# Decoder trunk on one core: the second mixer's causal mask moves from TensorE into VectorE's minimum, and its key-value latent is projected in plain fp32

## The chip, the cores and the metric

The kernel runs on one core of one Trainium2 chip. Its time is device microseconds (us) from one launch, the median of three runs. A profile of one further execution gives the span between the first and the last instruction, the busy time of each engine, and a record of each instruction. The engines are TensorE (PE, with PEld for its weight loads), VectorE (DVE), ScalarE (ACT), GpSimd (POOL), and SyncE (SP), which here only issues transfers.

## The reference, cut to what matters

Two layers, each a half-step SwiGLU FFN, a token mixer and another half-step FFN, for 256 tokens of width 1024 in float32. The first layer's mixer is a block-sparse attention with a learned bias (MoBA); the second layer's is a latent attention (MLA). Both have 16 heads. Only the second mixer changes:

```python
def mla_shared_kv(x, c_act, kv_ada_w, kv_ada_b, kv_norm_g, w_dkv, ...):
    hs = modulate(rms_norm(x, kv_norm_g), shift, scale)
    ckv_kpe = hs @ w_dkv                      # 256 x 1024 @ 1024 x 288
    ckv = rms_norm(ckv_kpe[..., :256], kv_a_norm_g)
    kpe = ckv_kpe[..., 256:]
    k_nope = (ckv @ w_uk).reshape(B, S, 16, 64)
    v = (ckv @ w_uv).reshape(B, S, 16, 64)
    ...
def mla_attention(h, w_dq, q_a_norm_g, w_uq, q_g, w_o, k, v, positions):
    q = (rms_norm(h @ w_dq, q_a_norm_g) @ w_uq).reshape(B, S, 16, 96)   # 1024 x 384, then 384 x 1536
    ...
    s = einsum("bqhd,bkhd->bhqk", q, k) * 96 ** -0.5
    s = where(kpos <= qpos, s, -1e30)
    o = einsum("bhqk,bkhd->bqhd", softmax(s), v)
    return o.reshape(B, S, 1024) @ w_o
```

## The kernel before

The work is one long list of instructions for the five engines. Tokens form two row tiles (`t` = 0, 1) of 128. Nearly every product is made of three fp32r matmuls: each float32 operand is split into a high part (`hi`, written by ACT) and a low part (`lo`, the rest, subtracted by DVE), and `mm3` (L799 to L803) issues hi·hi, lo·hi and hi·lo into the same PSUM bank. Weights come from HBM in the order of `weight_tiles` into a ring of three buffers (`raw`), and `wload` splits them, up to 1024 columns at a time, by an ACT copy (L678) and a DVE subtraction (L679). Modulation vectors (`ada`) are streamed through three further buffers (`adaw`).

The second mixer is `mla`. For each row tile it projects the normalized input `h` to the query latent (384 columns, L1478, records of `mm<-hi,h`) and the input `hkv`, which has its own norm and modulation, to the key-value latent (288 columns, `mm<-hi,hkv`). `q_norm`, run when the FFN before the mixer closes a row tile, has `modulate_cols` transpose the normalized rows (L850) and write `h` and `hkv`, each as a high and a low part by `split_evac` (ACT L815, DVE L816); before that split, the modulated `hkv` values stand in a tile `z`, which shares four buffers with the rows `y` to be transposed. `lat_norm_T` (L1438 to L1451) normalizes a latent, transposes it (L1448) and splits it into `qlT` or `ckT`. Then four groups `g` of four heads follow: `proj` makes their queries (`qn`) and keys (`kn`), `head_rstd` (ACT L1172, DVE L1175 and L1176, POOL's power at L1177) their norms, `to_T` transposes them (L1513), and `attention` scores, normalizes and applies them.

In `attention` a group has three score banks: `t` = 0 with four heads of 128 keys, and `t` = 1 with two banks of two heads of 256 keys. The scores are plain fp32 matmuls (L1080). For the second mixer one bf16 matmul per bank (L1081) then adds the causal mask, the identity times a tile of 0 and -1e30, DVE takes each bank's row maxima in one reduction, negated (L1094), and ACT takes exponentials out of PSUM with that as bias (L1105). The first mixer already does it another way: its scores have the opposite sign, DVE adds a bias head by head and takes the row minimum in the same instruction (L1098, recorded as CUSTOM_DVE_ANT_1), which writes the sum to SBUF, and ACT takes the exponential of the negated sum from there.

The order of instructions on each engine is set before the launch. `Order` holds every instruction with its dependencies and an estimated cost, places them by a list schedule that knows the buffers, the pools' life times and the transfers in flight, then tries variations of the due times drawn from the seeds in `TRIALS`, each drawn around the best order so far, and keeps a variation where its estimate of the end is earlier. So a change in any instruction can move instructions in the whole program, and each engine runs its own list strictly in that order. Transfers of weights are all on SP's queue, so one that waits for its buffer holds those behind it. A pool of tiles that is opened after another was closed may take its place in SBUF: its tiles are usable only after the last use of the closed one. The mixer's pool (`mla`) is opened so after the FFN's (`gp`, holding `gh` and `gl`).

Of the kernel before, what the change touches and what calls it, by code (L numbers as in the profile page):

```python
# [12 lines left out]
F32 = mybir.dt.float32  # L13
F32R = mybir.dt.float32r
# [76 lines left out]
def weight_tiles():  # L91


    for layer in range(2):
        for idx in range(2):
# [21 lines left out]
            else:  # L117
                for k0 in (0, 4):
                    yield [("mla_w_dq", (0,), 0)], k0, 4, QL
                for k0 in (0, 4):  # L120
                    yield [("w_dkv", (), 0)], k0, 4, KVL + RO
# [57 lines left out]
def bcast_row(ap, n, parts=P):  # L179
# [21 lines left out]
TRIALS = (30003, 30017, 30030, 30038, 30042, 30043, 30065, 30073, 30088, 30098, 30112, 30114, 30123, 30124, 30152,  # L201
          30165, 30226, 30230, 30319, 30491, 30718, 31097)
# [373 lines left out]
def trunk(ctx: ExitStack, tc: tile.TileContext, a: dict, out: bass.AP):  # L576
# [15 lines left out]
    def nm(s):  # L592
        uid[0] += 1
        return f"{s}_{uid[0]}"
# [58 lines left out]
    ident_b = cp.tile([P, P], BF16, name="ident_b")  # L653
    nc.vector.tensor_copy(ident_b, ident)
# [114 lines left out]

    def wload():  # L770


        parts, k0, kt, cols = next(wsrc)
        cols *= len(parts)
        raw = rawp.tile([P, kt * cols], F32, tag="raw", name=nm("raw"))
        n = P * kt * cols
        nc.sync.dma_start(raw, a["w"][wpos[0]:wpos[0] + n].rearrange("(p f) -> p f", p=P))
        wpos[0] += n
        per = max(1, 1024 // cols)
# [62 lines left out]
    def modulate_cols(t, r, keys, c0, n, wait):  # L842
# [4 lines left out]
        def fin():  # L847
# [4 lines left out]
            for i, (key, h) in enumerate(keys):  # L852
                z = tp.tile([P, n], F32, tag="y", name=nm("z"), bufs=4) if i else y
                step = n if c0 or i else P
                for c in range(0, n, step):
                    modulate(pt[:, c:c + step], z[:, c:c + step], key, (c0 + c) // P, step,
                             on_vector=i > 0 or len(keys) > 1 and t == 0 and c0 >= 512)
                    split_h(h, c0 + c, step, z[:, c:c + step])
# [31 lines left out]
    def hk(h, k):  # L890
        until(lambda: k in h[2])
        return h[0][:, k], h[1][:, k]
# [162 lines left out]
    def attention(ap, g, qTs, kTs, vs, bias, oT, state, after_s=None):  # L1055
# [7 lines left out]
        halves = bias is not None  # L1063
        UNITS = [(0, [0, 1, 2, 3]), (1, [0, 2] if halves else [0, 1]), (1, [1, 3] if halves else [2, 3])]

        def scores():
            until(lambda: state.get("av", 0) >= g)
            banks = []
            for t, es in UNITS:
# [9 lines left out]
                for i, e in enumerate(es):  # L1079
                    nc.tensor.matmul(ps3[:, i, :], qTs(e, t), kTs(e, nk), start=i == 0, stop=False)  # L1080
                nc.tensor.matmul(ps3[:, :, t * P:], ident_b, mask[:, :len(es)], start=False, stop=True)  # L1081
# [7 lines left out]
            for (t, es), ps3 in zip(UNITS, banks):  # L1089
# [3 lines left out]
                if bias is None:  # L1093
                    nc.vector.tensor_reduce(mx[:, :len(es)], ps3, axis=AX.X, op=ALU.max, negate=True)  # L1094
                else:
                    for i, e in enumerate(es):
                        s2, ps2 = [x.rearrange("p (b c k) -> p b c k", c=P // NB, k=NB) for x in (s3[:, i, :], ps3[i])]
                        nc.vector.tensor_tensor_reduce(s2, ps2, bias(t, e), 1.0, 3.0e38,  # L1098
                                                       op0=ALU.add, op1=ALU.min, accum_out=mx[:, i:i + 1])
# [636 lines left out]
```

## Time and profile before

| | us |
|---|---|
| median of three runs (lowest, highest) | 984.07 (983.84, 984.47) |
| time of the profiled execution | 984.34 |
| its span, first to last instruction | 982.6 |
| mean granted TensorE clock | 0.997 |

[...] How much of PE's time is issue is read from the distance between the starts of successive matmuls. In the records, a plain fp32 matmul counts twice. A row of the timeline gives start, length, engine, line, operation, output and inputs by the program's names, tile, shapes and count; several alike are merged into one row. In brackets stands how long the engine was idle before it and what ended that.

### The profile page before, as it was taken

The page shows a single profiled execution, that of the slowest core. Times are in us where ns is not written, and L with a number is a line of the kernel's source. Part 1 is how long each engine was busy: PE and PEld are TensorE (multiplying, and loading weights), DVE is VectorE, ACT ScalarE, POOL GpSimd, SP SyncE. Part 2 cuts the span into 40 slices and gives each one's busy share as a digit, 9 for nine tenths or more (in the row PEclk, how much of TensorE's full clock was granted, in tenths as well). Part 3 has the DMA queues.
Part 4 walks back from the last instruction along what each step waited for, and adds up shares of the span by engine and source line. Part 5 has one row for each costly group of instructions (what it writes and reads, how often), then busy time and mean ns, then how long its engine had stood idle before and what let it go on. Part 6 is the DMA issues. An engine that isn't in the chain of part 4 may idle for free.

```text
span 982.6 us, 15317 instructions
## 1 busy us (share of the span) xinstructions
PE 970.8 (99%) x5556; PEld 829.0 (84%) x5559; DVE 834.4 (85%) x1478; ACT 616.7 (63%) x1162; POOL 85.5 (9%) x120
## 2 busy tenths in 40 slices
PE   8999999999999999999999999999999999999998
PEld 6998888888888788888878888888888778888887
DVE  7999999798899999999799999964899689667642
ACT  5689564378666966555367665643979696666521
POOL 1012000012240100000010000000143110000000
PEclk8999999999999999999999999999999999999999
DMA  9968989798787798889789899962344377644630
GB/s 366 409 248 280 384 325 349 273 350 327 276 299 257 254 356 334 312 336 353 289 326 338 308 342 339 325 248 89 108 157 171 130 256 270 220 176 172 235 129 21
DMA packets 54282, 263.72 MB, mean 268 GB/s; under 512 B 6304, under 2 KB 7104, under 8 KB 36032
## 3 DMA queue, kind: packets, MB, share of 16 engines
q1 hardware_dynamic: 51840, 255.93, 70.6%
q0 software_dynamic: 1888, 6.32, 2.2%
q8 instruction: 43, 0.70, 0.3%
q10 hardware_dynamic: 480, 0.51, 0.2%
q14 instruction: 31, 0.25, 0.1%
HBM read 258.52 MB, written 4.22 MB: 267 GB/s over the span
## 4 chain that ended last, share of the span: by engine, by line
PE 89%; DVE 4%; DMA 4%; ACT 1%; POOL 1%; issue 1%; SPq 0%; POOLq 0%; DVEq 0%; ACTq 0%
PE mm L1005 26%; PE mm L800 14%; PE mm L801 14%; PE mm L802 14%; PE mm L1013 14%; DMA raw<-in_first_dram 4%; PE at L1140 1%; PE tr L850 1%; PE tr L1242 1%; PE at L1120 1%; DVE lo L679 1%; POOL hr L1177 1%; PE at L1085 1%; PE tr L1513 0%; DVE mx L1094 0%
## 5 line engine op out<-in xcount | busy, mean ns | idle before, releaser
L679 DVE TENSOR_TENSOR lo<-raw,hi 128x1024 fp32r<-128x1024 f32 (+3 forms) x312 | 369.2, 1200 | 80.6 <-ACT hi L678 65.1
L678 ACT ACTIVATE hi<-raw 128x1024 fp32r<-128x1024 f32 (+3 forms) x312 | 316.2, 1037 | 135.3 <-PE mm L802 103.9
L1005 PE MATMUL mm<-h,hi 128*128 128x512 f32 x1120 | 268.1, 391 | 0.0
L1005 PEld LDWEIGHTS mm<-h,hi 128*128 128x128 f32 x1120 | 205.7, 188 | 39.7
L692 DVE CUSTOM_DVE_ANT_0 adaw<-adaw,c_b,cols 128x1024 f32<-128x1024 f32 x160 | 203.3, 1284 | 2.5 <-ACT raw L1628 1.6
L1013 PEld LDWEIGHTS mm<-h,lo 128*128 128x128 f32 x1120 | 144.4, 191 | 5.5
L1013 PE MATMUL mm<-h,lo 128*128 128x256 f32 x1120 | 148.3, 284 | 0.0
L800 PE MATMUL mm<-hi,gh 128*128 128x512 f32 (+1 forms) x356 | 138.2, 388 | 0.0
L801 PE MATMUL mm<-lo,gh 128*128 128x512 f32 (+1 forms) x356 | 137.7, 387 | 0.0
L802 PE MATMUL mm<-hi,gl 128*128 128x512 f32 (+1 forms) x356 | 137.7, 387 | 0.0
L800 PE MATMUL mm<-hi,h 128*128 128x512 f32 (+1 forms) x240 | 95.2, 400 | 0.0
L801 PE MATMUL mm<-lo,h 128*128 128x512 f32 (+1 forms) x240 | 93.4, 392 | 0.0
L802 PE MATMUL mm<-hi,h 128*128 128x512 f32 (+1 forms) x240 | 91.6, 391 | 0.0
L801 PEld LDWEIGHTS mm<-lo,gh 128*128 128x128 f32 x356 | 66.9, 188 | 13.4
L802 PEld LDWEIGHTS mm<-hi,gl 128*128 128x128 f32 x356 | 66.9, 188 | 13.5
L800 PEld LDWEIGHTS mm<-hi,gh 128*128 128x128 f32 x356 | 66.9, 188 | 13.3
L815 ACT ACTIVATE gh<-g 128x256 fp32r<-128x256 f32 x76 | 31.2, 412 | 53.0 <-DVE g L948 52.7
L800 PEld LDWEIGHTS mm<-hi,h 128*128 128x128 f32 x240 | 44.9, 188 | 9.7 <-issue 1.3
L802 PEld LDWEIGHTS mm<-hi,h 128*128 128x128 f32 x240 | 45.1, 188 | 9.3 <-DVE h L816 0.5
L801 PEld LDWEIGHTS mm<-lo,h 128*128 128x128 f32 x240 | 45.2, 188 | 7.6 <-issue 0.2
L944 ACT ACTIVATE g<-mm 128x256 f32<-128x256 f32 x70 | 26.4, 378 | 34.3 <-PE mm L1013 31.5
L1177 POOL TENSOR_TENSOR hr<-hv,mhalf 128x4 f32<-128x4 f32 (+1 forms) x24 | 41.0, 1708 | 63.1 <-DVE hv L1176 53.9
(234 smaller groups left out, 1164.6 us busy)
## 6 DMA issues: line engine op xcount, KB each, us to landing
raw<-in_w_dram SPq DMA_DIRECT2D x142, 1024.0 KB, 6.3
adaw<-in_ada_dram SPq DMA_DIRECT2D x160, 512.0 KB, 6.2
raw<-in_w_dram SPq DMA_DIRECT2D x12, 512.0 KB, 3.9
raw<-in_first_dram SPq DMA_DIRECT2D x7, 512.0 KB, 9.2
raw<-in_w_dram SPq DMA_DIRECT2D x6, 576.0 KB, 3.9
bias_d<-bt SPq DMA_DIRECT2D x12, 256.0 KB, 3.9
gate<-gate_d POOLq DMA_DIRECT2D x6, 512.0 KB, 6.7
bg<-bias_d POOLq DMA_DIRECT2D x4, 768.0 KB, 5.9
```

The lines of the kernel that those rows point to most:

```text
L678: nc.scalar.activation(hi, src, AF.Copy)
L679: nc.vector.tensor_tensor(lo, src, hi.bitcast(F32), op=ALU.subtract)
L692: nc.vector.tensor_tensor_reduce(wt, wt, c_b, 1.0, start, op0=ALU.mult, op1=ALU.add, accum_out=col)
L800: nc.tensor.matmul(ps, lh, rh, start=start, stop=False)
L801: nc.tensor.matmul(ps, lh, rl, start=False, stop=False)
L802: nc.tensor.matmul(ps, ll, rh, start=False, stop=stop)
L815: nc.scalar.activation(hi, ps, AF.Copy)
L850: nc.tensor.transpose(kslice(pt, j), kslice(y, j), ident)
L944: nc.scalar.activation(x, ps[:, S:], AF.Copy)
L1005: nc.tensor.matmul(ps[i], w[0], hs[2], start=k == 0, stop=False)
L1013: nc.tensor.matmul(*low[:3], start=False, stop=low[3])
L1177: nc.gpsimd.tensor_tensor(r, v2, mhalf[:, :nh], op=ALU.pow)
```

## The change

The mask is now a float32 tile of 0 and 1e30, 256 columns wide, shared by all heads. The query gain carries the opposite sign, so the second mixer's scores are negated like the first's, and DVE's one instruction per head adds the mask and takes the minimum; the twelve mask matmuls, the twelve reductions and the bf16 identity are gone. ACT's exponentials read SBUF.

The key-value latent's input `hkv` is one float32 tile (`h[1]` is None), written straight by the modulation, without `z` and without a split; its weight `w_dkv` comes in three tiles of 3, 3 and 2 blocks of 128 rows (864, 864 and 576 columns) rather than two of four blocks, not into the `raw` ring but into three tiles of the mixer's pool that later hold queries and keys (`homes`), and is not split. Each block of 128 rows is one plain fp32 matmul of 288 columns instead of three fp32r matmuls. The seeds are new.

```diff
-                for k0 in (0, 4):
-                    yield [("w_dkv", (), 0)], k0, 4, KVL + RO
+                for k0 in range(0, KD, 3):
+                    yield [("w_dkv", (), 0)], k0, min(3, KD - k0), KVL + RO
...
-TRIALS = (30003, 30017, 30030, 30038, 30042, 30043, 30065, 30073, 30088, 30098, 30112, 30114, 30123, 30124, 30152,
+TRIALS = (100001, 100005, 100024, 100026, 100027, 100035, 100043, 100107, 100144, 100150, 100174, 100330, 100345,
...
-    ident_b = cp.tile([P, P], BF16, name="ident_b")
-    nc.vector.tensor_copy(ident_b, ident)
...
+        plain = parts[0][0] == "w_dkv"
         cols *= len(parts)
-        raw = rawp.tile([P, kt * cols], F32, tag="raw", name=nm("raw"))
+        raw = homes.pop(0)[:, :kt * cols] if plain else rawp.tile([P, kt * cols], F32, tag="raw", name=nm("raw"))
...
+        if plain:
+            return [raw[:, k * cols:(k + 1) * cols] for k in range(kt)]
...
-                z = tp.tile([P, n], F32, tag="y", name=nm("z"), bufs=4) if i else y
+                z = y
+                if h[1] is None:
+                    z = h[0][:, c0 // P:(c0 + n) // P].rearrange("p k q -> p (k q)")
+                    h[2].update(range(c0 // P, (c0 + n) // P))
...
-                    split_h(h, c0 + c, step, z[:, c:c + step])
+                    if h[1] is not None:
+                        split_h(h, c0 + c, step, z[:, c:c + step])
...
-                    nc.tensor.matmul(ps3[:, i, :], qTs(e, t), kTs(e, nk), start=i == 0, stop=False)
-                nc.tensor.matmul(ps3[:, :, t * P:], ident_b, mask[:, :len(es)], start=False, stop=True)
+                    nc.tensor.matmul(ps3[:, i, :], qTs(e, t), kTs(e, nk), start=True, stop=True)
...
-                if bias is None:
-                    nc.vector.tensor_reduce(mx[:, :len(es)], ps3, axis=AX.X, op=ALU.max, negate=True)
-                else:
...
+                for i, e in enumerate(es):
+                    s2, ps2 = s3[:, i, :], ps3[i] if halves else ps3[:, i, :]
+                    if halves:
+                        s2, ps2 = [x.rearrange("p (b c k) -> p b c k", c=P // NB, k=NB) for x in (s2, ps2)]
+                    nc.vector.tensor_tensor_reduce(s2, ps2, bias(t, e), 1.0, 3.0e38,
+                                                   op0=ALU.add, op1=ALU.min, accum_out=mx[:, i:i + 1])
...
-                    nc.scalar.activation(ss[u][:, i, :], (banks if bias is None else ss)[u][:, i, :], AF.Exp,
-                                         bias=mxs[u][:, i:i + 1], scale=1.0 if bias is None else -1.0,
+                    nc.scalar.activation(ss[u][:, i, :], ss[u][:, i, :], AF.Exp, bias=mxs[u][:, i:i + 1], scale=-1.0,
...
-    mask = cp.tile([P, GH, P], BF16, name="mask")
+    mask = cp.tile([P, S], F32, name="mask")
...
-        for nme, mul in (("q", QK ** -0.5), ("k", 1.0)):
+        for nme, mul in (("q", -QK ** -0.5), ("k", 1.0)):
...
+            homes.extend(ap.tile([P, GH * S], F32, tag=g, name=nm("wkv")) for g in ("qT", "qT", "kT"))
...
-                        mm3(ps[:, :n], *hk(src[t], k), *pls[i][k], start=k == 0, stop=k == KD - 1)
+                        if i:
+                            mm3(ps[:, :n], *hk(src[t], k), *pls[i][k], start=k == 0, stop=k == KD - 1)
+                        else:
+                            nc.tensor.matmul(ps[:, :n], hk(src[t], k)[0], pls[i][k], start=k == 0, stop=k == KD - 1)
...
-                              lambda e, kb: vs[g][:, kb, e * DH:(e + 1) * DH], None, oT, state)
+                              lambda e, kb: vs[g][:, kb, e * DH:(e + 1) * DH],
+                              lambda t, e: mask[:, (1 - t) * P:], oT, state, False)
...
-        parts = [adap.tile([P, D], F32R, tag="acc" if t and g else "adaw", name=nm("hkv"), bufs=1 if t and g else 3)
-                 for g in range(2)]
-        hkv[t] = *[x.rearrange("p (k q) -> p k q", q=P) for x in parts], set()
+        z = adap.tile([P, D], F32, tag="adaw", name=nm("hkv"))
+        hkv[t] = z.rearrange("p (k q) -> p k q", q=P), None, set()
```

The order moves at three places that matter here. Lines are some numbers higher in the changed program (L800 to L802 become L803 to L805, L850 becomes L853, L1513 becomes L1521). On PE, at the end of the first row tile's query projection (`mm_7595` before) the key-value projection follows (`mm_7648`), before:

```order
L802 MATMUL mm_7595<-hi_7602,h_7470 128x384
L850 MATMUL tr_7665<-ident,y_7574 128x128 x2
L801 MATMUL mm_7648<-lo_7621,hkv_7468 128x288
L802 MATMUL mm_7648<-hi_7620,hkv_7469 128x288
L800 MATMUL mm_7648<-hi_7620,hkv_7468 128x288
```

and after, where `wkv` are the three unsplit weight tiles, `mm_7626` is the key-value projection and the `y` are the second row tile's normalized rows:

```order
L805 MATMUL mm_7582<-hi_7589,h_7467 128x384
L1485 MATMUL mm_7626<-wkv_7579,hkv_7466 128x288 x3
L853 MATMUL tr_7630<-ident,y_7558 128x128
L853 MATMUL tr_7642<-ident,y_7560 128x128
L853 MATMUL tr_7654<-ident,y_7562 128x128 x2
L853 MATMUL tr_7642<-ident,y_7560 128x128
L853 MATMUL tr_7630<-ident,y_7558 128x128
L853 MATMUL tr_7675<-ident,y_7564 128x128 x2
L1485 MATMUL mm_7626<-wkv_7580,hkv_7466 128x288 x3
L1485 MATMUL mm_7626<-wkv_7581,hkv_7466 128x288 x2
```

The second row tile's transposes, spread over the key-value projection before, now stand together between its first three and its last five matmuls.

On SP's queue, at the same place, before (`raw_7618` and `raw_7649` are the two halves of `w_dkv`; then come the first group's query weights, its key-value weights and the second group's query weights):

```order
L777 DMA raw_7618<-in_w_dram 128x1152
L777 DMA raw_7649<-in_w_dram 128x1152
L777 DMA raw_7697<-in_w_dram 128x1152
L777 DMA raw_7855<-in_w_dram 128x1024
L777 DMA raw_7912<-in_w_dram 128x1152
```

and after:

```order
L778 DMA raw_7664<-in_w_dram 128x1152
L778 DMA raw_7781<-in_w_dram 128x1024
L778 DMA wkv_7579<-in_w_dram 128x864
L778 DMA wkv_7581<-in_w_dram 128x576
L778 DMA wkv_7580<-in_w_dram 128x864
L778 DMA raw_7838<-in_w_dram 128x1152
```

The three loads of `w_dkv` have moved behind the first group's weights (`raw_7664`, `raw_7781`) and ahead of the second group's.

On PE, at the last group's keys (`kn_8432` before, `kn_8362` after), the second half of the transposes and what follows, before:

```order
L800 MATMUL mm_8556<-hi_8564,h_7854 128x512
L801 MATMUL mm_8556<-lo_8565,h_7854 128x512
L1513 MATMUL tr_8621<-ident,kn_8432 96x128 x4
L1140 MATMUL at_8633<-pT_8585,v_8300 64x128 x2
L1140 MATMUL at_8633<-pT_8592,v_8300 64x128 x4
```

and after (`mm_8488` is the output projection, `at_8526` the transposed probabilities of the third group):

```order
L803 MATMUL mm_8488<-hi_8492,h_7780 128x512
L1123 MATMUL at_8526<-ident,s_8407 128x128 x4
L1521 MATMUL tr_8547<-ident,kn_8362 96x128 x4
L804 MATMUL mm_8488<-lo_8493,h_7780 128x512
L1521 MATMUL tr_8553<-ident,kn_8362 96x128 x4
L805 MATMUL mm_8488<-hi_8492,h_7780 128x512
```

Between the last projection of these keys and this second half of their transposes stood 23 matmuls of 512 columns and 24 transposes before; now it is 17 such matmuls, 44 transposes, the second group's 12 matmuls of probabilities with values, and the third group's whole score block of eight fp32 matmuls.

More of the change, by code (lines that the diff above doesn't have):

```diff
@@ L199 @@
 ROUND_OF_ORDER = 4
-TRIALS = (30003, 30017, 30030, 30038, 30042, 30043, 30065, 30073, 30088, 30098, 30112, 30114, 30123, 30124, 30152,
-          30165, 30226, 30230, 30319, 30491, 30718, 31097)
+TRIALS = (100001, 100005, 100024, 100026, 100027, 100035, 100043, 100107, 100144, 100150, 100174, 100330, 100345,
+          100624, 100719, 100918, 100952, 101026, 101035, 101823, 101924, 102566, 103950, 105379, 105559, 105767)
 ENGINES = ("PE", "DVE", "Activation", "Pool", "SP")
@@ L768, in trunk @@
     wq, wpos = [], [0]
+    homes = []
     def wload():
         parts, k0, kt, cols = next(wsrc)
+        plain = parts[0][0] == "w_dkv"
         cols *= len(parts)
-        raw = rawp.tile([P, kt * cols], F32, tag="raw", name=nm("raw"))
+        raw = homes.pop(0)[:, :kt * cols] if plain else rawp.tile([P, kt * cols], F32, tag="raw", name=nm("raw"))
         n = P * kt * cols
@@ L891, in hk @@
         until(lambda: k in h[2])
-        return h[0][:, k], h[1][:, k]
+        return h[0][:, k], h[1] is not None and h[1][:, k]
     def hk_both(h, k):
@@ L1052, in ffn, with attention @@
             after(1)
-    def attention(ap, g, qTs, kTs, vs, bias, oT, state, after_s=None):
+    def attention(ap, g, qTs, kTs, vs, bias, oT, state, halves, after_s=None):
         pT, ss, sms = {}, [], []
-        halves = bias is not None
         UNITS = [(0, [0, 1, 2, 3]), (1, [0, 2] if halves else [0, 1]), (1, [1, 3] if halves else [2, 3])]
@@ L1092, in scores @@
                 mx = small([P, 4], "mx")
-                if bias is None:
-                    nc.vector.tensor_reduce(mx[:, :len(es)], ps3, axis=AX.X, op=ALU.max, negate=True)
-                else:
[L1096 to L1099, printed above, removed]
+                for i, e in enumerate(es):
[4 more added lines that the diff above has]
+                                                   op0=ALU.add, op1=ALU.min, accum_out=mx[:, i:i + 1])
                 ss.append(s3)
@@ L1356, in to_T @@
                     lambda t, e: bg[g][:, t:2 * t + 1, :, e * NB:(e + 1) * NB],
-                    oT, state, lambda: g + 1 < NG and load_bias(g + 1))
+                    oT, state, True, lambda: g + 1 < NG and load_bias(g + 1))
             for t in range(NT):
@@ L1420, in mla_consts @@
         nc.gpsimd.memset(mask, 0.0)
-        nc.gpsimd.affine_select(mask, mask, pattern=[[0, GH], [-1, P]], compare_op=ALU.is_ge, fill=NEG, base=0,
+        nc.gpsimd.affine_select(mask, mask, pattern=[[-1, S]], compare_op=ALU.is_ge, fill=-NEG, base=P,
                                 channel_multiplier=1)
@@ L1477, in mla @@
                             pls[i] += nextw()
-                        mm3(ps[:, :n], *hk(src[t], k), *pls[i][k], start=k == 0, stop=k == KD - 1)
+                        if i:
+                            mm3(ps[:, :n], *hk(src[t], k), *pls[i][k], start=k == 0, stop=k == KD - 1)
+                        else:
+                            nc.tensor.matmul(ps[:, :n], hk(src[t], k)[0], pls[i][k], start=k == 0, stop=k == KD - 1)
+                            pe(0.49)
                     if i:
@@ L1508, in to_T @@
             def to_T(g, kind, nat, gcol, then):
-                dst = ap.tile([QK, GH, S], F32, tag=kind + "T", name=nm(kind + "T"))
+                dst = ap.tile([P, GH * S], F32, tag=kind + "T", name=nm(kind + "T"))[:QK].rearrange("p (e q) -> p e q", e=GH)
                 for t in range(NT):
```

## The prediction

> **What bounds the kernel now.** I read the page's engine totals first, then its chain, then the busy time by stage.
>
> ```profile
> PE 970.8 (99%) x5556; PEld 829.0 (84%) x5559; DVE 834.4 (85%) x1478; ACT 616.7 (63%) x1162; POOL 85.5 (9%) x120
> PE 89%; DVE 4%; DMA 4%; ACT 1%; POOL 1%; issue 1%; SPq 0%; POOLq 0%; DVEq 0%; ACTq 0%
> 10.00:15.00 5.00, 3.90 (x26) 3.59 (x26) 4.15 (x9) 3.77 (x9) 0.00 (x0) 0.58 1.04 416
> 700.00:720.00 20.00, 19.31 (x119) 17.58 (x118) 19.23 (x56) 17.07 (x47) 6.12 (x7) 1.00 0.34 113
> 720.00:740.00 20.00, 19.51 (x130) 16.80 (x129) 18.79 (x50) 17.00 (x43) 7.59 (x6) 1.00 0.54 187
> 740.00:760.00 20.00, 19.89 (x137) 17.18 (x138) 19.32 (x42) 18.91 (x52) 7.36 (x5) 1.00 0.41 159
> 760.00:780.00 20.00, 18.60 (x127) 15.13 (x127) 15.59 (x32) 14.88 (x38) 4.71 (x2) 1.00 0.30 106
> ```
>
> PE is busy for 970.8 of 982.6 us and makes 89% of the chain that ended last. The second mixer is the one long stage where three engines are full at once: from 700 to 760 us DVE is busy 57.3 of 60 us and ACT 53.0 (columns: PE, PEld, DVE, ACT, POOL, then granted clock, share of DMA, GB/s). PE sets the pace there too, but waits now and then for a result that went through DVE and ACT. So an edit here can gain in two ways only: PE work taken away, and PE waits taken away. The timeline shows the four longest waits, each as the distance to the next row's start:
>
> ```profile
> 693.38 0.40 PE L802 MATMUL mm<-hi,gl 128*128 128x512 f32 x1
> 696.97 0.33 PE L800 MATMUL mm<-hi,h 128*128 128x384 f32 x1
> 697.83 0.34 PE L802 MATMUL mm<-hi,h 128*128 128x384 f32 x1
> 698.01 0.38 PE L850 MATMUL tr<-ident,y 128*128 128x128 f32 x2
> 698.86 0.40 PE L801 MATMUL mm<-lo,hkv 128*128 128x288 f32 x1 [0.47 <-DVE lo L679]
> 699.10 0.30 PE L802 MATMUL mm<-hi,hkv 128*128 128x288 f32 x1
> 700.29 0.30 PE L802 MATMUL mm<-hi,hkv 128*128 128x288 f32 x1
> ...
> 716.20 0.38 PE L1448 MATMUL tr<-ident,ly 128*128 128x128 f32 x2
> 717.11 0.50 PE L800 MATMUL mm<-hi,ckT 128*128 128x512 f32 x1 [0.53 <-ACT ckT L815]
> ...
> 731.41 0.28 PE L1081 MATMUL at<-mask,ident_b 128*128 128x256 bf16 x1
> 732.18 0.50 PE L1513 MATMUL tr<-ident,qn 128*96 128x128 f32 x3 [0.49 <-DVE rs L1110]
> ...
> 766.37 0.39 PE L800 MATMUL mm<-hi,h 128*128 128x512 f32 x1
> 766.60 0.39 PE L801 MATMUL mm<-lo,h 128*128 128x512 f32 x1
> 768.07 0.61 PE L1513 MATMUL tr<-ident,kn 128*96 128x128 f32 x4 [1.08 <-DVE kn L1548]
> ```
>
> A transpose takes 0.11 us of issue (four are 0.23 longer than two, 768.07 against 698.01), an fp32r matmul of 512 columns 0.23 (766.37 to 766.60). The two transposes at 698.01, 0.22 us of issue, were followed after 0.85: 0.63 us lost, to the low part of `w_dkv`. The others lost 0.69 (0.91 less 0.22), 0.66 (0.77 less 0.11) and 1.24 us (1.47 less 0.23); smaller ones, not shown, add about 1 us. So all waits in the mixer are worth some 4.2 us, 0.4% of the kernel.
>
> **The change part by part.** First the mask matmuls. The last two groups' blocks have their rows side by side:
>
> ```profile
> 727.59 0.38 PE L1081 MATMUL at<-mask,ident_b 128*128 128x512 bf16 x1
> 727.62 0.53 PE L800 MATMUL mm<-hi,qlT 128*128 128x384 f32 x1
> 727.99 0.34 PE L801 MATMUL mm<-lo,qlT 128*128 128x384 f32 x1
> ...
> 772.20 0.27 PE L1081 MATMUL at<-mask,ident_b 128*128 128x256 bf16 x1
> 772.31 1.03 PE L1080 MATMUL at<-kT,qT 96*128 96x256 f32 x4
> 773.18 0.27 PE L1081 MATMUL at<-mask,ident_b 128*128 128x256 bf16 x1
> ...
> L1080 PEld LDWEIGHTS at<-kT,qT x64: 186/190/193, 726.5 to 772.7; 96*128 96x128 f32 x64
> ```
>
> From 727.59 to 727.99 PE issued one 512-column mask and one 384-column fp32r matmul. Such a matmul takes 0.172 us (five steps from 696.97 to 697.83), so the mask took 0.23. A 256-column mask took 0.11 (772.20 to 772.31). Four and eight of them: 4 x 0.23 + 8 x 0.11 = 1.8 us less on PE, at full price, since PE paces.
>
> Then the key-value projection. Before, 48 fp32r matmuls of 288 columns: nine steps between 699.10 and 700.29 make 0.132 us each, 6.34 us. After, 16 plain fp32 ones, of which each counts twice. No such width is in the trace; the nearest is the score matmul of 256 columns, four records from 772.31 to 773.18, 0.2175 us each. Scaled by 288/256 that is 0.245 a record, 0.49 a matmul, 7.83 us in all: PE gets 1.5 us more. Bounds: if a record's time didn't grow with its columns, 32 x 0.2175 = 6.96 us, 0.6 more than before; were the two 0.19 us weight loads of each (last row) no longer hidden, 32 x 0.19 = 6.1 on top. The scores hide theirs in the same way, so I take the scaled row. The mask and the projection together leave PE 0.3 us less work. Changing between fp32r and fp32 costs nothing I can see in the 727.59 rows, which contain such a change, so the order of kinds is not priced.
>
> DVE and ACT lose the splits:
>
> ```profile
> L679 DVE TENSOR_TENSOR lo<-raw,hi 128x864 fp32r<-128x864 f32 x2 | 2.1, 1050 | 0.0
> L816 DVE TENSOR_TENSOR hkv<-z,hkv 128x256 fp32r<-128x256 f32 x8 | 3.4, 419 | 0.0
> L815 ACT ACTIVATE hkv<-z 128x256 fp32r<-128x256 f32 x8 | 3.3, 412 | 0.2
> L1094 DVE TENSOR_REDUCE mx<-at x12: 681/684/693, 728.8 to 773.5; 128x2 f32<-128x512 f32 x8, 128x4 f32<-128x512 f32 x4
> L1098 DVE CUSTOM_DVE_ANT_1 s<-at,bg x24: 284/420/426, 238.8 to 304.0; 128x256 f32<-128x256 f32 x16, 128x128 f32<-128x128 f32 x8
> ```
>
> In the latent projections DVE loses 2.1 + 3.4 = 5.5 us, and ACT at least 3.3; the splits of the last 288 columns and ACT's side of the weights come on top. In the groups DVE gets eight instructions for three: 4 x 0.284 + 4 x 0.42 = 2.8 against 3 x 0.684 = 2.05 us, 0.8 more a group, 3.1 in all. DVE thus comes out at least 2.4 us lighter and has its relief ahead of its load. None of this is on PE's path itself, where PE has work in hand; the cover for the extra 0.8 us is, in the last group, the output projection's matmuls that stand between scores and transposes (19 of 512 columns before, 21 after). Were it gone, that group would end 0.8 us later. ACT's exponentials can start after the first head's minimum (0.284) instead of a whole bank's reduction (0.684), so the chain from scores to probabilities gets no longer.
>
> The waits. The one at 698.01 goes with the split it waited for: 0.6 us. For the others I go by the order. The keys of the last group have room for 23 x 0.23 + 24 x 0.11 = 7.9 us of PE work between projection and last transposes before, and for 17 x 0.23 + 44 x 0.11 = 8.8 and a score block and the values besides after, so I take its 1.24 us as gone. The tile at 717.11 follows its transposes directly before; after, four matmuls of the other row tile come between, 0.9 us, more than the 0.69 lost, so I count that too. The one at 731.41 has much the same surroundings in both orders; with less work queued on DVE I count half, 0.3, and 0.2 of the small ones. That is 0.6 + 1.24 + 0.7 + 0.3 + 0.2 = 3.0 us less waiting. A new order has waits of its own that no row can show; the nearest guide are the old one's, 4.2 us, of which I put 1.0 us as new ones.
>
> The new loads. The `wkv` tiles lie in the mixer's pool, so they can be issued only when the FFN's last matmul (693.38) has ended at 693.78. Landing is bounded by these rows:
>
> ```profile
> ga_q<-in_mla_q_a_norm_g_dram ACTq DMA_DIRECT2D x1, 192.0 KB, 3.1
> raw<-in_w_dram SPq DMA_DIRECT2D x6, 576.0 KB, 3.9
> raw<-in_w_dram SPq DMA_DIRECT2D x2, 768.0 KB, 4.5
> raw<-in_first_dram SPq DMA_DIRECT2D x7, 512.0 KB, 9.2
> ```
>
> The first tile has 432 KB, between the first two rows: 3.6 us, so 697.4 on the old time scale. PE first needs it after the query projection, 24 x 0.172 = 4.1 us, and two transposes behind 693.6, at 697.9. All three hold 1152 KB; beyond the 768 KB row at the 416 GB/s of the first window shown they land in some 5.4 us, 699.2, and the second tile is needed three fp32 matmuls and eight transposes later, at 700.3. So the loads are hidden, by 0.5 and 1.1 us, and cost nothing in the sum. What waits behind them on SP's queue are the second group's weights, needed only after the first group's projections. The `adaw` buffer that becomes free isn't used: neither order has an `ada` transfer in the mixer.
>
> The rest of the program is only reordered by the new seeds. PE waits little there except in the first 20 us, where the granted clock is 0.58 in one window; a shift of the moment at which it returns would be worth up to 0.42 x 5 = 2.1 us in either direction. I take 0.
>
> Sum: 0.3 us of work and 3.0 us of waits less, 1.0 us of new waits, so -2.3 us. The profiled execution took 984.34 us, 0.27 above the median of the three; from it I get 982.0, from the median 981.8, and forecast 981.8.
>
> **The rivals.** No measurable change, within 0.2% (1.97 us, about what a measurement of this kernel can tell from none; so 982.1 to 986.0): the waits come back at other places. What speaks for it is how the longest one arose:
>
> ```profile
> 764.04 2.35 DVE L679 TENSOR_TENSOR lo<-raw,hi 128x1024 fp32r<-128x1024 f32 x2
> 764.08 3.19 POOL L1177 TENSOR_TENSOR hr<-hv,mhalf 128x4 f32<-128x4 f32 x1 [1.28 <-DVE hv L1176]
> ...
> 755.74 1.01 POOL L1177 TENSOR_TENSOR hr<-hv,mhalf 128x4 f32<-128x4 f32 x1 [0.81 <-DVE hv L1176]
> ```
>
> POOL's power of four numbers takes 1.01 us alone and 3.19 beside two of DVE's 1024-column subtractions, and PE then waited 1.24 us for the keys. All the 1024-column subtractions stay, in another order. Where one such meeting recurs with a consumer close behind, 1.2 us of the gain is lost; where the queries' wait at 731.41 stays whole too, 0.3 more: -0.8 us, 983.3. [...]
>
> Slower: the `wkv` loads land late. Place: the first fp32 matmul of the projection. Each us after 697.9 is a us of idle PE. The 512 KB tiles at the start, with the DMA engines full, took 9.2 us: then the matmul could start at 703.0, 5.1 us late, and the time would be 986.9. From a landing of 8.3 us on it decides for slower than 0.2%. Against it: DMA is at 0.34 in that stage.
>
> That the new projection doesn't do what it says, with its weight loads exposed, is the other slower case: 981.8 + 6.1 = 987.9; against it, the score rows above.
>
> **How the numbers follow.** Gain as summed or more: 0.53, with a range of its own from 979.6 (no new waits, the last 1.2 us of old waits gone too) to 982.1. Same, by recurring waits or a few tenths of wait for the loads: 0.37. Late loads: 0.07. Exposed weight loads: 0.03. So faster 0.53, same 0.37, slower 0.10. The range of 8 in 10 leaves out the slower cases and a tenth beyond the low end and runs from 979.6 to 984.4.
>
> **What would show it.** In the changed profile: no L1081 rows; 32 records of `mm<-wkv,hkv` at a distance of 0.245 us; no wait for a `lo` of `w_dkv`; a `wkv` landing within 4.1 us of its issue and no idle time before the first of its matmuls; the tile maxima in eight DVE rows of 0.28 and 0.42 us a group; POOL's powers near 1 us; and the mixer, from the FFN's last matmul to 780 us, some 2 us shorter while the stages on either side keep their lengths. I am wrong if the waits in the mixer still sum to over 3 us, if PE idles for `wkv`, or if the first 20 us shift.

## The result, and the profile after

| | before | after |
|---|---|---|
| median (lowest, highest), us | 983.96 (983.73, 984.47) | 978.15 (978.11, 978.25) |
| ratio, 95% interval | | 0.994, 0.9923 to 0.9958 |
| span of the profiled execution, us | 982.6 | 976.4 |

The change makes the kernel 5.8 us faster, where 2.3 were forecast; 978.15 lies below the range of 979.6 to 984.4. The engine totals and the chain of the page after, then the busy time by stage (columns PE, PEld, DVE, ACT, POOL, granted clock, DMA share, GB/s):

```profile
PE 966.7 (99%) x5531; PEld 827.3 (85%) x5531; DVE 838.6 (86%) x1517; ACT 613.6 (63%) x1150; POOL 80.1 (8%) x120
PE 93%; DMA 4%; DVE 1%; ACT 1%; POOL 0%; issue 0%; ACTq 0%; SPq 0%; DVEq 0%
```

```profile
10.00:15.00 5.00, 4.41 (x40) 4.22 (x41) 4.49 (x8) 3.74 (x9) 0.00 (x0) 1.00 1.03 411
700.00:720.00 20.00, 19.84 (x102) 17.01 (x101) 17.61 (x51) 15.24 (x41) 4.89 (x7) 1.00 0.43 144
720.00:740.00 20.00, 20.00 (x135) 18.02 (x135) 19.37 (x65) 18.44 (x45) 9.87 (x8) 1.00 0.42 150
740.00:760.00 20.00, 20.00 (x149) 17.61 (x145) 18.76 (x71) 17.62 (x52) 6.95 (x6) 1.00 0.14 53
760.00:780.00 20.00, 20.00 (x140) 16.73 (x139) 15.84 (x36) 14.78 (x35) 0.00 (x0) 1.00 0.56 211
```

From 720 to 780 us PE is never without a matmul in flight; before, it was busy 58.0 of 60 us there. The chain is PE at 93% instead of 89%, and DVE's share of it fell from 4% to 1%. From 10 to 20 us the clock is full here (1.00 in both windows); before, the windows 10:15 and 15:20 had 0.58 and 0.74.

To see where the time came from I cut both traces at the same events of PE, by the starts of matmuls:

| stage | before | after | difference |
|---|---|---|---|
| up to the first FFN's second half of columns | 50.58 | 50.22 | -0.36 |
| to its last down matmul | 159.58 | 159.36 | -0.22 |
| first mixer and gate part of the next FFN | 236.94 | 236.43 | -0.51 |
| second FFN's down matmuls, third FFN up to its own | 185.35 | 184.75 | -0.60 |
| third FFN's down matmuls | 60.93 | 60.59 | -0.34 |
| second mixer and fourth FFN up to its down matmuls | 224.96 | 220.94 | -4.02 |
| the rest | 59.90 | 59.90 | 0.00 |

The fifth row belongs to the mixer: before, two matmuls of its query projection (0.35 us) stood among the last down matmuls. So the mixer gave 4.4 us and everything ahead of it 1.7.

Inside the mixer, the timeline's rows at the end of the FFN and at the key-value projection:

```profile
691.35 0.39 PE L805 MATMUL mm<-hi,gl 128*128 128x512 f32 x1
695.81 0.34 PE L805 MATMUL mm<-hi,h 128*128 128x384 f32 x1
697.05 1.70 PE L1485 MATMUL mm<-wkv,hkv 128*128 128x288 f32 x6 [0.90 <-DMA wkv<-in_w_dram]
698.59 1.04 PE L853 MATMUL tr<-ident,y 128*128 128x128 f32 x8
...
708.13 2.11 PE L1485 MATMUL mm<-wkv,hkv 128*128 128x288 f32 x8
710.08 0.83 PE L1451 MATMUL tr<-ident,ly 128*128 128x128 f32 x4
```

The loads of `wkv`, by their tile, with first and last issue and the time to landing:

```profile
L778 SPq DMA_DIRECT2D wkv<-in_w_dram x3: 328/424/426, 691.8 to 692.6; - x3
DMA to landing us min/median/max: 5.1/6.0/6.6
```

DVE's minima (shortest, median, longest in ns), and POOL's powers in the second mixer alone (busy us, mean ns, idle time before):

```profile
L1102 DVE DVE_READ_ACCUMULATOR2_ANT mx<- x64: 75/82/86, 238.0 to 769.3; 128x1 f32 x64
L1102 DVE CUSTOM_DVE_ANT_0 s<-at,mask x32: 278/344/425, 728.0 to 768.9; 128x128 f32<-128x128 f32 x16, 128x256 f32<-128x256 f32 x16
L1180 POOL TENSOR_TENSOR hr<-hv,mhalf 128x4 f32<-128x4 f32 x16 | 20.1, 1258 | 26.2 <-DVE hv L1179 26.2
```

The first `wkv` tile is issued when the FFN has ended, as foreseen, but needs 5.1 us and not 3.6: PE stands for 1.07 us (695.81 to 697.05, less 0.17). That is the late-load rival at a fifth of its size, and the price is in the 978.15. Eight records of the new projection take 1.95 us, 0.244 each. All old waits of the prediction's list are gone.

To divide the 4.4 us, I took from every distance between matmul starts what its shape issues in (0.2275, 0.1735, 0.132 us for 512, 384, 288 columns, 0.2445 for a `wkv` record, and so on, and what a change of kind shifts from one distance into the next: from 701.16 to 702.06 three `wkv` records and a 384-column matmul take 0.90 us, what the four issue in, but 0.39 of it stands behind the start of the last). A record is longer than its issue: 0.33 us for 384 columns. What remains is waiting: 9.4 us before and 5.0 after in the stage of the second mixer. (What one counts as issue moves both sums together, by up to 4 us, and their difference by a few tenths.) The work itself differs by a few tenths. So the mixer's gain is PE waits, and the experiments ask whose merit that is: the changed instructions', or that of the order which the new seeds found.

### The profile page after: what moved, and what is told of

Read it like the earlier page. It is cut to its first block, busy times and chain, and to the rows that moved or that the text cites. A ratio compares the mean times of both kernels' runs of the same rounds, so it can differ in the third digit from the quotient of the medians.

```text
span 976.4 us, 15274 instructions
## 1 busy us (share of the span) xinstructions
PE 966.7 (99%) x5531; PEld 827.3 (85%) x5531; DVE 838.6 (86%) x1517; ACT 613.6 (63%) x1150; POOL 80.1 (8%) x120
## 4 chain that ended last, share of the span: by engine, by line
PE 93%; DMA 4%; DVE 1%; ACT 1%; POOL 0%; issue 0%; ACTq 0%; SPq 0%; DVEq 0%
PE mm L1012 26%; PE mm L803 15%; PE mm L804 15%; PE mm L805 15%; PE mm L1020 14%; DMA raw<-in_first_dram 3%; PE at L1143 1%; PE at L1086 1%; PE at L1123 1%; PE tr L1245 1%; PE tr L853 1%; PE mm L1485 1%; PE tr L1521 1%; PE at L1090 1%; DMA wkv<-in_w_dram 1%; DMA cols<-in_cols_dram 1%
## 5 line engine op out<-in xcount | busy, mean ns | idle before, releaser
L677 DVE TENSOR_TENSOR lo<-raw,hi 128x1024 fp32r<-128x1024 f32 (+1 forms) x308 | 366.2, 1206 | 69.7 <-ACT hi L676 55.7
L676 ACT ACTIVATE hi<-raw 128x1024 fp32r<-128x1024 f32 (+1 forms) x308 | 315.0, 1042 | 136.6 <-PE mm L805 118.8
L803 PE MATMUL mm<-hi,gh 128*128 128x512 f32 (+1 forms) x356 | 138.2, 388 | 0.0
L805 PE MATMUL mm<-hi,gl 128*128 128x512 f32 (+1 forms) x356 | 137.6, 387 | 0.0
L803 PE MATMUL mm<-hi,h 128*128 128x512 f32 (+1 forms) x240 | 93.9, 399 | 0.0
L805 PE MATMUL mm<-hi,h 128*128 128x512 f32 (+1 forms) x240 | 91.9, 391 | 0.0
L805 PEld LDWEIGHTS mm<-hi,gl 128*128 128x128 f32 x356 | 66.9, 188 | 13.7
L803 PEld LDWEIGHTS mm<-hi,gh 128*128 128x128 f32 x356 | 66.9, 188 | 13.1
L803 PEld LDWEIGHTS mm<-hi,h 128*128 128x128 f32 x240 | 45.1, 188 | 9.4 <-issue 1.0
L805 PEld LDWEIGHTS mm<-hi,h 128*128 128x128 f32 x240 | 45.1, 188 | 8.6
```

Of the source, the lines that this page charges most:

```text
L676: nc.scalar.activation(hi, src, AF.Copy)
L677: nc.vector.tensor_tensor(lo, src, hi.bitcast(F32), op=ALU.subtract)
L803: nc.tensor.matmul(ps, lh, rh, start=start, stop=False)
L805: nc.tensor.matmul(ps, ll, rh, start=False, stop=stop)
```

## The experiments

All times are medians of runs beside the kernel before (983.9 to 984.0 in each series). "Written out" means that each engine's list of instructions stands in the kernel as a table, so that an edit moves nothing else.

**New seeds alone, old seeds, no seeds.**

```diff
 b_new: before,  TRIALS = (100001, 100005, ... 105767)
 a_old: after,   TRIALS = (30003, 30017, ... 31097)
 b0:    before,  TRIALS = ()
 a0:    after,   TRIALS = ()
```

> The kernel before with the new seeds and nothing else. By the two traces the mixer (from the FFN's last matmul to the first matmul of the next FFN) became 4.0 us shorter, and the stretches before it together 2.0. Theory A (the mixer's part comes from the changed instructions, the rest from the new order): the seeds alone move the time by one to two us in either direction, 982.5 to 986, and the mixer stays within 1.5 us of its 124.1. Theory B (most of the 5.8 us comes from a better order found by the new seeds): 981 or less. Theory C (orders hardly matter, all of the gain is the change): 984.0 within 0.5.

> The changed kernel with the seeds of before. Theory A: the mixer keeps about 4 us of gain whatever the order, the rest is one to two us of luck: 978.5 to 981. Theory B: 983 or more. Theory C: 978.2 within 0.5.

> The kernel before with an empty list of seeds: the list schedule without any variation. Theory A: up to 3 us above before, 984 to 987, spread over the stages. Theory C: 984.0 within 0.5. It is the base for the changed kernel without variations.

> The changed kernel with an empty list of seeds. Theory A: 3 to 5 us below the kernel before with an empty list, nearly all of it in the mixer. Theory B: within 1.5 us of it. Theory C: 5.3 to 6.3 us below it.

| | no seeds | other kernel's seeds | own seeds |
|---|---|---|---|
| before | 986.00 | 985.93 | 983.96 |
| after | 987.40 (984.92 to 988.34) | 986.71 (984.63 to 988.44) | 978.15 |

None of the three theories holds. The new seeds do nothing for the old kernel, so B falls, though its numbers for `a_old` and `a0` come true; A's come true for `b_new` and `b0` alone, for without seeds of its own the changed kernel is slower than the old one, 1.4 us with no seeds. The trace without seeds shows a first reason. PE's rows at the first `wkv` matmul, and windows of 6, 7 and 6 us around it:

```profile
696.26 0.34 PE L804 MATMUL mm<-hi,h 128*128 128x384 f32 x1
698.59 2.26 PE L1484 MATMUL mm<-wkv,hkv 128*128 128x288 f32 x4 [1.99 <-DMA wkv<-in_w_dram]
...
700.71 0.67 PE L802 MATMUL mm<-hi,h 128*128 128x384 f32 x1
701.18 0.52 PE L803 MATMUL mm<-lo,h 128*128 128x384 f32 x1
701.50 0.52 PE L804 MATMUL mm<-hi,h 128*128 128x384 f32 x1
```

```profile
692.00:698.00 6.00, 3.98 (x21) 3.05 (x19) 5.73 (x17) 5.02 (x11) 0.77 (x1) 0.98 0.82 249
698.00:705.00 7.00, 6.41 (x19) 5.17 (x20) 3.18 (x6) 2.46 (x7) 0.00 (x0) 0.53 0.71 232
705.00:711.00 6.00, 6.00 (x35) 5.48 (x33) 5.40 (x16) 5.88 (x17) 1.51 (x2) 1.00 0.01 3
```

PE waits 2.2 us for `wkv` (696.26 to 698.59, less 0.17), and then the granted clock is half: 384-column matmuls come every 0.32 us instead of 0.17. What is missing from full clock in the first two windows, 0.02 x 6 and 0.47 x 7, makes 3.4 us of lost PE work, that is 6.8 us at half clock. The spread of the times, 984.92 to 988.34, is as large, and each execution's mean granted clock goes with it: the two at 1.000 took 984.92 and 985.79, the four at 0.997 and 0.998 took 987.24 to 988.34. So it is the halved clock that makes the changed kernel without seeds the slower one; where the clock holds it lies 0.2 to 1.1 us below the kernel before without seeds.

The place on SP's queue is one difference. Without seeds, the next group's weights (576 KB) stand ahead of the `wkv` tiles; in the changed kernel's own order they stand behind. The first tile is issued when the FFN has ended in both, but lands after 5.8 us (692.63 to 698.45) instead of 5.1, and PE comes to it 0.4 us sooner after its issue.

**Each part alone, without seeds.** `m0` has the mask on DVE, with `w_dkv` split and three fp32r matmuls as before; `p0` has the plain projection, with the mask matmuls on PE.

> The mask part alone: the kernel before with DVE adding the mask, w_dkv split and projected by three fp32r matmuls as before, and no seeds; base is the kernel before without seeds (986.0). If the mask part is worth the PE work it removes and a wait at a mask row: 2 to 3 us less, 983 to 984, all of it in the mixer. If it brings DVE work onto the path instead: 986 or more.

> The projection part alone: w_dkv loaded unsplit into the mixer's pool and projected in plain fp32, mask on PE as before, no seeds; base 986.0. Theory L (late loads: PE idles for wkv some 2 us, and the granted clock then drops to 0.5 for several us, as it did in the changed kernel with the old seeds and with none): 988 to 991, with a granted clock of 0.5 somewhere from 698 to 706 us. Theory W (the projection itself is what the new order paid for): 985 to 986.5 with the clock at 1.0.

Measured: 984.13 for the mask part, a little above its range and 1.9 us below the kernel before without seeds; 987.82 (986.45 to 988.34) for the projection part, 1.8 above it and just under theory L's range. The projection part again waits 2.2 us for `wkv`, with a granted clock of 0.50 from 698 to 701 us and 0.83 in the next. The mechanism of theory L holds for it (four of five executions have a clock of 0.997 or 0.998; the one at 1.000 is the 986.45), and the mask part gives what PE loses in work.

**The load alone: earlier and later.** The changed kernel's own order, written out.

```diff
 f_early
-            homes.extend(ap.tile([P, GH * S], F32, tag=g, name=nm("wkv")) for g in ("qT", "qT", "kT"))
+            homes.append(adap.tile([P, D], F32, tag="adaw", name=nm("wkv")))
+            homes.extend(ap.tile([P, GH * S], F32, tag=g, name=nm("wkv")) for g in ("qT", "kT"))
 SP: +wkv_0  raw (1024 columns)  -wkv_0  wkv_2  wkv_1  raw (1152 columns)
 f_late
 SP: raw (1024 columns)  +raw (1152 columns)  wkv_0  wkv_2  wkv_1  -raw (1152 columns)
```

> The changed kernel with its own order written out as a table of positions, and one edit: the first of the three wkv tiles lies in the modulation buffer that the change freed, and its transfer stands one place earlier on SP's queue, ahead of the last weight tile before it, so that it lands before the FFN ends. Theory L: PE's wait of 0.90 us before the first matmul on wkv goes and nothing replaces it: 977.0 to 977.5. Rival (the second tile or the hkv input is late next): 977.7 to 978.2.

> The changed kernel with its own order written out, and one edit: on SP's queue the next group's weight tile (576 KB) stands ahead of the three wkv tiles instead of behind them. Theory L with a cliff: the wait for wkv grows by 1.4 us or more, to above 2 us, and the granted clock drops to 0.5 after it for 3 to 7 us, so 981 to 984. Rival, without a cliff: only the longer wait, 979.5 to 980.5, clock at 1.0.

Measured: 977.23 (977.00 to 977.55; against before 0.9932, 0.9916 to 0.9948) and 980.93 (979.68 to 981.75). PE's rows with the early load, and then with the late one and its clock:

```profile
695.84 0.33 PE L811 MATMUL mm<-hi,h 128*128 128x384 f32 x1
696.01 1.62 PE L1492 MATMUL mm<-wkv,hkv 128*128 128x288 f32 x6
697.46 1.05 PE L859 MATMUL tr<-ident,y 128*128 128x128 f32 x8
698.62 2.18 PE L1492 MATMUL mm<-wkv,hkv 128*128 128x288 f32 x8
```

```profile
695.83 0.34 PE L811 MATMUL mm<-hi,h 128*128 128x384 f32 x1
698.69 2.87 PE L1491 MATMUL mm<-wkv,hkv 128*128 128x288 f32 x6 [2.52 <-DMA wkv<-in_w_dram]
```

```profile
695.00:699.00 4.00, 1.48 (x8) 1.15 (x7) 3.56 (x7) 2.25 (x6) 1.40 (x1) 1.00 0.97 332
699.00:703.00 4.00, 4.00 (x15) 3.15 (x14) 0.18 (x1) 0.18 (x1) 0.00 (x0) 0.57 0.90 357
703.00:707.00 4.00, 4.00 (x20) 3.25 (x19) 3.04 (x11) 3.97 (x14) 0.00 (x0) 1.00 0.00 0
```

Early, the wait is gone at its price (0.92 us), and this is the fastest kernel of the study. Late, the wait grows from 0.90 to 2.52 us, which alone makes 979.8; the clock at 0.57 in four us loses 0.43 x 4 = 1.7 us more (3.4 us at half clock), 981.5. The six executions lie at both ends: 981.44, 981.58 and 981.75, all with a mean clock of 0.998, and 979.68, 979.81 and 980.41, of which the last two have 1.000. By these times and clocks the cliff is there in half of them (the profiled one, 981.44, shows it), and the median falls between the ranges of theory L and its rival.

**The early load without seeds.** The orders of `a0` and `p0`, written out, with the same edit of home, the first `wkv` tile early on SP's queue, and the other two ahead of the next group's weights.

> The changed kernel in the order that it has without seeds (987.4), written out, with only SP's queue changed: the first wkv tile lies in the freed modulation buffer and is loaded ahead of the last weight tile before the mixer, and the other two stand ahead of the next group's weights instead of behind them. Theory L (what spoils the change without seeds is the late load and the halved clock after it): the trace without seeds shows 2.2 us of PE idle and 6.6 us at a granted clock of 0.5, together 5.5 us, so 981.5 to 983, which is 3 to 4.5 us below the kernel before without seeds (986.0). Rival (without the seeds the change gains nothing even when the loads are early): 985 to 986.5.

> The projection part alone in its order without seeds (987.8), with the same edit on SP's queue. The trace shows 2.2 us idle and 3.8 us at half clock, together 4.1: theory L 983 to 984.3, 2 to 3 us below the kernel before without seeds. Rival (the plain projection's 1.5 us of PE work eats what it saves in waits): 985.5 to 986.5.

Measured: 985.56 and 985.65, clock 1.0. Both rivals hold: only 0.4 us below the kernel before without seeds. The rows of `a0_early` show what came instead:

```profile
700.58 0.38 PE L859 MATMUL tr<-ident,y 128*128 128x128 f32 x2
702.33 0.45 PE L809 MATMUL mm<-hi,h 128*128 128x384 f32 x1 [1.37 <-ACT h L824]
```

With the 2.2 us filled, PE reaches the second row tile's matmuls before their input is written, and waits 1.6 us for that. The late load had hidden it. So theory L explains the cliff, but not the gain of the tuned order: 985.56 is no better than the executions of `a0` in which the clock held.

**The mask matmuls put back.** The changed kernel's order, written out, with twelve bf16 matmuls of the identity and a tile of zeros behind the score matmuls.

```diff
-                    nc.tensor.matmul(ps3[:, i, :], qTs(e, t), kTs(e, nk), start=True, stop=True)
+                    nc.tensor.matmul(ps3[:, i, :], qTs(e, t), kTs(e, nk), start=i == 0, stop=False)
+                nc.tensor.matmul(ps3[:, :, t * P:], ident_b, nothing[:, :len(es)], start=False, stop=True)
```

> The changed kernel in its own order, written out, with twelve bf16 matmuls of the identity and a tile of zeros put back behind the score matmuls where the mask matmuls were (and two small POOL instructions that make the tiles). If the mask matmuls were on PE's path at full price: 1.8 us more, 979.8 to 980.1. Rival (the mixer's waits hide part of them): 978.6 to 979.3.

Measured: 979.93 (979.88 to 980.20), 1.78 us more than the changed kernel. Full price, nothing hidden.

**A wait far from the change.** The order before, written out, with two transposes moved three matmuls back.

> The kernel before in its own order, written out, with one edit on PE at 513 us, in the third FFN, far from the change: two transposes that waited 0.53 us for rows from ACT stand three matmuls later. If the 0.6 us that the changed kernel gained between 507 and 532 us is this order alone: 983.4 to 983.6. Rival (the wait moves to the next consumer of the transposed rows): 983.9 to 984.1.

Measured: 983.82 against 984.01, ratio 0.9999 (0.9990 to 1.0008). The rows before; after the move; and a window at the start after the move:

```profile
513.23 0.40 PE L802 MATMUL mm<-hi,h 128*128 128x512 f32 x1
513.98 0.44 PE L850 MATMUL tr<-ident,y 128*128 128x128 f32 x2 [0.35 <-ACT y L845]
```

```profile
513.64 0.38 PE L856 MATMUL tr<-ident,y 128*128 128x128 f32 x2
514.27 0.50 PE L806 MATMUL mm<-hi,h 128*128 128x512 f32 x1 [0.25 <-ACT h L821]
```

```profile
10.00:15.00 5.00, 3.90 (x36) 3.69 (x37) 4.29 (x9) 3.94 (x9) 0.00 (x0) 1.00 1.04 415
```

The wait moved to the next reader; the stage became 0.09 us shorter. So the 0.6 us of that stage isn't the place of these two transposes. Every kernel with the projection part has it, whatever its seeds (184.7 to 184.8 us for the stage, against 185.3 to 185.4), and all of these have the eight pairs of transposes of that stretch at the same places among the matmuls, five of them at others than before. The kernel before with the long search (below) has a third order there, lacks the wait, and takes 184.9. So another order of the whole stretch is worth at least some 0.4 of the 0.6 us, though this move isn't; why the schedule takes it with the projection part, even without seeds, stays open. The window at the start shows something else: in the same order the clock was full from 10 to 15 us here, where it was 0.58 in the profile before, and the first event of the stage table came at 50.11 instead of 50.58. The start differs between executions of one order, so most of the 0.36 us of the first stage is no merit of the change. Nor is it the clock's: `m0` and `a_old`, whose clock is full there, reach that event at 50.74.

**How long the order was searched.** The seeds of before reach over some 1,100 numbers, those of after over 5,800. `b_more` searches the kernel before over some 5,400, `a_cut` keeps only the changed kernel's first 1,100, `m_more` and `p_more` give each part alone the long search; a seed is kept where the kernel's own schedule estimates an earlier end.

> The kernel before with 38 seeds instead of 22: the 22 it had and 16 more from the next 4,700 numbers that improve its schedule's own estimate of the end. The spread of the new seeds (100001 to 105767) suggests that the changed kernel's order was searched over some 5,800 numbers, the old one's over 1,100; here both have had the same. Theory S (a part of the 5.8 us is the longer search): 982 to 983.3. Rival (the old order was as good as it gets): 983.7 to 984.3.

> The changed kernel with only the first 19 of its 26 seeds, those up to 101035, which is a search as short as the one of the kernel before. wkv stands ahead of the next group's weights on SP's queue here too, so no cliff. Theory S: 0.5 to 1.2 us above the changed kernel, 978.6 to 979.4. Rival (the last seeds brought nothing real): 978.0 to 978.3. A third way, that the wait for wkv grows to 2 us and the clock drops: above 981.

> The mask part alone with 19 seeds found by the same long search. The PE work removed is 1.8 us, and in the run without seeds the mask part alone gave 1.9. If the mask part keeps its gain in a searched order: 1.3 to 2.3 us below the kernel before with as long a search, 980.3 to 981.7 if that comes out at 982.6. Rival (a searched order hides what is left and the parts end alike): within 0.7 us of it.

> The projection part alone with 34 seeds found by the same long search. On SP's queue the next group's weights still stand ahead of the wkv tiles. Theory L: the wait for wkv and the halved clock after it stay, so 984 to 987, whatever the seeds. Rival: the searched order covers the landing with other PE work: 982 to 983.5.

| | measured | against before |
|---|---|---|
| kernel before, long search | 985.48 | +1.5 |
| mask part alone, long search | 981.99 | -2.0 |
| projection part alone, long search | 981.72 (981.28 to 983.61) | -2.3 |
| both, short search | 979.30 | -4.7 |
| both, long search (after) | 978.15 | -5.8 |

The long search did not help the kernel before: its schedule expected an earlier end and the chip gave a later one, outside both ranges of `b_more`. Its trace loses in the first mixer's stage (238.3 us against 236.9) and is 0.5 us shorter in the second's. So the advantage is not bought by searching longer, except for the last 1.15 us, which `a_cut` lacks, within theory S. `m_more` was forecast relative to `b_more` and lies 3.5 us below it, outside both its ranges. With an order searched for it, each part gives about two us against the best order of the kernel before, and the two nearly add up: 4.3 of 5.8 us. The 1.5 between are less than one order differs from another in the unchanged kernel (983.96 to 986.00). For the same reason these runs, each with one order, don't show the share of each part; for the mask's matmuls `f_mask` does.

The waits of the second mixer's stage say more. Counted with the median distance of each pair of kinds as issue (an estimate from these traces), they are 9.4 to 10.0 us in the unchanged kernel's orders (`before`, `b0`, `b_more`), 8.4 with the mask part and a long search, 7.7 with the projection part and a long search, of which 1.9 are for `wkv`, and 5.7 with both. That points to the projection part for most of the waits that vanished, and only in an order searched for it: in `a0_early`, with the load early and no seeds, they are 12.0. One order each doesn't prove it.

For the projection part theory L failed and its rival came nearer (981.72 lies below even its 982), though its load is as late as without seeds:

```profile
696.72 0.81 PE L854 MATMUL tr<-ident,y 128*128 128x128 f32 x6
699.24 4.12 PE L1490 MATMUL mm<-wkv,hkv 128*128 128x288 f32 x16 [1.70 <-DMA wkv<-in_w_dram]
```

```profile
699.00:703.00 4.00, 3.76 (x16) 3.00 (x17) 2.85 (x10) 2.09 (x7) 0.55 (x1) 1.00 0.48 156
```

The search put six of the second row tile's eight transposes ahead of the wait, and sixteen records in one run behind it; 1.9 us are still lost, but the clock held in this execution. Of the eleven, nine have a mean clock of 0.999 or 1.000 and take 981.28 to 981.96; the two at 0.998 and 0.996 take 983.19 and 983.61.

## Why the prediction was wrong, step by step

- Mask matmuls, 1.8 us of PE at full price: right (1.78 with them put back). The two blocks shown for it are the first and the last group's, not the last two.
- Projection, 0.245 us a record and 1.5 us more PE work: right (0.244; the weight loads, 0.19 us each, stayed hidden). That rival is refuted.
- DVE at least 2.4 us lighter: off. It lost 6.4 us of splits and 8.2 of reductions, and got 10.4 us of minima and, which I had left out, after each minimum a read of its accumulator of 0.08 us (the L1102 rows), 2.6 us for 32 of them: 1.6 us lighter by these rows, while DVE's total on the page rose from 834.4 to 838.6 us. The chain has DVE at 1%, so it was hardly on the path.
- The four long waits, of which I counted 2.8 of 3.2 us: all gone. Right. The first went with its split, as reasoned; that the other three went is the merit of the tuned order, for the same instructions without seeds wait no less than the kernel before (12.0 us against 10.0 even with the load early).
- The smaller waits: here the sum failed. I put all of the mixer's waits at 4.2 us, took 0.2 of the small ones, and 1.0 us as new. What I didn't list was nearer 6 us than 1 (9.4 less the four), because waits under 0.2 us were taken for issue; the stage went from 9.4 to 5.0 us of waiting, some 4.3 net where I had 2.0. The 1.0 us of new waits was right in size by luck: it was meant for waits of the new order, and what came is the wait for `wkv`, which I had counted as nothing.
- `wkv` hidden by 0.5 us: wrong, late by 1.1 us. The 3.6 us came from rows between which its size lay; the row of the same queue in this stage measures 5.1 to 6.6. I priced the rival per us of landing, 1 for 1; in `f_late` the halved clock added 1.7 us to a wait of 2.5, and in `a0` 3.4 to one of 2.0, which the rival didn't have.
- The rest of the program at 0: wrong by 1.7 us. I named the first twenty us as the risk; they gave 0.36 of it, mostly chance. (I priced them from the one window shown; with the 0.74 of the next the lost clock is 3.4 us of work, not 2.1.) The remainder lies in the first mixer (0.5), the third FFN (0.6) and the first FFN (0.2); of the first mixer's, orders alone move it by over a us (236.9 to 238.3 in the kernels with the old projection).
- POOL's powers near 1 us: right for most. Of the sixteen in the second mixer nine take 1.00 to 1.02 us, the mean is 1.26 and the longest 2.05, where before the longest took 3.19.

The step that failed is thus the treatment of the order, in two terms of the sum: the small waits, put at 0.2 us, so that the mixer's waits shrank by some 4.3 us net where the sum had 2.0, and the rest of the program, put at 0, which gave 1.7. Together they are what the forecast was short of, 2.3 against 5.8 us (6.2 between the two profiled executions). I summed four waits, guessed 1.0 us for new ones and set the rest to zero, although the schedule is searched anew for each program. The runs show that the order alone moves the unchanged kernel from 983.96 to 986.00 and the changed one from 978.15 to 987.40, the latter, without seeds, with a mean clock of 0.997 or 0.998 in four of six executions and the halved clock in the profiled one.

What remains open: which of the small waits went with which instruction, why the third FFN is ordered otherwise with the projection part, and why the schedule's estimate was wrong about the kernel before with more seeds.

## What to carry to other kernels

A change to a kernel whose order is searched has two prices: one for its instructions, read from rows, and one for its order, which runs of the old and the new kernel with and without seeds bound before anything is concluded. Of PE's waits in a saturated stage, add up all distances beyond issue, not the rows with a bracket. And place a load that stands ahead of PE by its queue: one tile ahead of it was the difference between a wait of 0.9 us and one of 2.5 us, behind which the clock was 0.57 for four us in the profiled execution (by the times, in three of six).

## What the runs showed of the hardware

In the profiled executions of `a_old`, `a0`, `p0` and `f_late`, PE stood idle for 1.9 to 2.5 us before the first matmul on `wkv`, and the granted clock dropped to 0.5 there: for 3.4 us in three of them, 1.7 us of lost work (in `f_late` 0.57 from 699 to 703 us), and for 6.8 us in `a0` (0.53 from 698 to 705 us). In the 3.4 us before the drop, a piece as long as those three drops, PE had stood for 1.8 to 2.5 us in all, in `a0` in two pieces (0.6 and 1.2). After idle times of 0.9 us (the changed kernel), 1.4 (`a0_early`) and 1.7 (`p_more`, in its profile) it did not drop; between 100 and 970 us no 3.4 us of these last three profiles hold more than that 1.7. One order had it in some executions and not in others: of the six of `a0`, four have a mean clock of 0.997 or 0.998, and two have 1.000. The runs show no more than these figures, so neither from which idle time on the clock drops nor what sets the length of a drop.
